# A two-layer decoder with eight experts on one core: the small group's silu is ordered behind the splits of the large group's down weights

## The chip, the core and the metric

The kernel runs on one core of a Trainium2 chip. TensorE (PE, with its weight loads shown apart as PEld) does the matmuls, ScalarE (ACT) and VectorE (DVE) do the elementwise work, GpSimd (POOL) is nearly unused, and SyncE (SP) issues the transfers of the weights from HBM. The metric is the time of the whole kernel on the device in microseconds, as the median of its runs; smaller is better.

## What is computed

Two decoder layers over 256 tokens of width 1024, in float32. Each layer has attention, and then a channel mixer: a dense SwiGLU of inner width 3584 in the first layer, and in the second one eight such SwiGLU experts, of which each token uses two. Of the reference only the mixers matter here:

```python
def swiglu(h, wg, wu, wd):
    return (jax.nn.silu(h @ wg) * (h @ wu)) @ wd

def moe_swiglu(h, router, wg, wu, wd):
    logits = (h @ router).astype(jnp.float32)
    top_vals, top_idx = lax.top_k(logits, TOP_K)          # TOP_K = 2 of 8
    gates = jax.nn.softmax(top_vals, axis=-1)
    ...
    for e in range(N_EXPERTS):
        out = out + gate_e[..., e:e + 1] * swiglu(h, wg[e], wu[e], wd[e])
    return out
```

## The kernel before

The change lies in the second layer's mixer. An expert's tokens are gathered into 128, 64 or 32 slots. Experts are taken in eight turns, 0 to 7. Turns 0, 2, 4, 5 and 6 have 128 slots and are the **large** ones (class `Ffn`); turns 1 and 7 have 64 slots and turn 3 has 32, and these are the **small** ones (class `Few`). Each expert's inner width is cut into seven groups of 512 columns. A group's work is: `gate` (a product over 1024, then silu on ACT), `up` (a product, then a multiplication by the silu on DVE), `turn` (transposes on PE, copied out of PSUM by ACT and, for a large one, by DVE) and `down` (the product with the down weights, summed up in PSUM over the seven groups).

A list of steps, written by hand, mixes the groups: small groups of turn 1 stand among those of 0 and 2, those of turn 3 among 2 and 4 (mostly one small after two large), and those of turn 7 alternate with those of 6. Turn 5 runs alone. A step of group n does `gate(n)`, `turn(n-1)`, `up(n)`, `down(n-1)`. So where a small group follows a large one, PE does in this order: the small gate, the large group's four transposes, the small up, the large group's down.

Weights come as tiles of 1 MiB (128 x 2048 float32), two each for a group's gate, up and down, 336 for the eight experts. They come in a ring of 14 buffers, in the order of use; a tile's transfer is issued when the tile 14 places ahead of it has been used up. A small group multiplies the float32 tile as it is. A large group splits each half of a tile into two parts: ACT writes `whi` (rounded), DVE writes `wlo` (what the rounding left), and PE multiplies three times, `whi` and `wlo` with the high part of the activations and `whi` with the low part. `whi` and `wlo` have four buffers each, so at most four split halves are ahead of PE; a half is six matmuls of 512 columns, so a large gate, up or down has four halves and 24 matmuls.

A scheduler in the tile framework puts each engine's instructions in an order before the program is built. ACT and DVE work through theirs in that order. `tc.issue_after(ins)` is a wish to that scheduler: whatever is recorded in its block comes behind `ins`, if it is on the same engine as `ins`; it adds no wait on a semaphore. The lines that the rows below name are L290 (`whi` on ACT), L291 (`wlo` on DVE), L337 to L339 (the three matmuls), L607 and L616 (silu and multiplication of a large group), L624, L627 and L628 (its transposes, `aTh` on ACT, `aTl` on DVE), L675 (small gate and up), L681 and L684 (silu and multiplication of a small group), L690 and L692 (its transposes and `aTh`) and L702 (small down).

Of the kernel before, what the change touches and what calls it, by code (L numbers as in the profile page):

```python
# [10 lines left out]
F32 = mybir.dt.float32  # L11
# [3 lines left out]
AF = mybir.ActivationFunctionType  # L15
ALU = mybir.AluOpType
# [3 lines left out]
P = 128  # L20
# [76 lines left out]
def trunk(ctx: ExitStack, tc: tile.TileContext, a: dict, out: bass.AP):  # L97
    nc = tc.nc
    V, A, G, T = nc.vector, nc.scalar, nc.gpsimd, nc.tensor
# [160 lines left out]


    ring = [wraw] * RAW
    free, behind = [0], []
    turn = [0]

    def more_raw():
# [14 lines left out]
    def split(raw, shape, q):  # L281
        hi = wsp.tile([P, 1024], F32R, name="whi")
        lo = wsp.tile([P, 1024], F32R, name="wlo")
        half = raw[:, 1024 * q : 1024 * q + 1024]
        with ExitStack() as es:
            free[0] -= 1
            if free[0] < 0:
                for ins in behind:
                    es.enter_context(tc.issue_after(ins))
            A.activation(hi, half, AF.Copy)  # L290
            V.tensor_tensor(lo, half, hi.bitcast(F32), op=ALU.subtract)  # L291
        return [x.rearrange("p (a b) -> p a b", a=shape[0] // 2) for x in (hi, lo)]

    def by_quarter(src, shape):
# [8 lines left out]
    def weight(src, shape):  # L303
        raw = load(src, shape)
        return [split(raw, shape, q) for q in range(2)]

    class Stream:
# [6 lines left out]
        def more(self):  # L314

            while sum(x[1] is not None for x in self.ready) < self.lead and len(self.ready) < 12 + self.lead:
                if not self.raw:
                    t = next(self.tiles, None)
                    if t is None:
                        return  # L320
                    if t[2:] == (QUARTERS,):
                        self.ready += by_quarter(*t[:2])
                        return
                    raw = load(*t[:2])
                    self.raw = [(raw, t[1], q, t[2:]) for q in range(2)]
                raw, shape, q, whole = self.raw.pop(0)
                if whole:
                    half = raw[:, 1024 * q : 1024 * q + 1024]
                    self.ready.append((half.rearrange("p (a b) -> p a b", a=shape[0] // 2), None))
                else:  # L330
                    self.ready.append(split(raw, shape, q))
# [27 lines left out]
    with tc.tile_pool(name="rope0", bufs=1) as rp:  # L359
# [8 lines left out]
        for bits in (8, 9, 9):  # L368
            e = math.floor(math.log2(rest)) + 1 - bits
# [207 lines left out]
    class Ffn:  # L577
# [23 lines left out]
        def gate(self, g):  # L601
            def done(t, ps):
                s = self.s[g, t] = self.sp.tile([P, GW], F32, name="silu", bufs=2 * self.nt)
                if self.rs is None:
                    A.activation(s, ps, AF.Silu)
                else:
                    A.activation(s, ps, AF.Silu, scale=self.rs(t))  # L607
            self.product(self.wg, g, done)
# [46 lines left out]
    class Few:  # L655
# [22 lines left out]

        def gate(self, g):
            s = self.s[g] = self.sp.tile([P, self.nj * P], F32, name="silu", bufs=2)  # L680
            A.activation(s, self.product(), AF.Silu, scale=self.rs)  # L681

        def up(self, g):
            V.scalar_tensor_tensor(self.s[g], self.product(), self.rs, self.s[g], op0=ALU.mult, op1=ALU.mult)  # L684
# [52 lines left out]
    def moe(i, norm, make_next):  # L737
# [74 lines left out]
        with ExitStack() as es:  # L812
            sp = es.enter_context(tc.tile_pool(name=f"mo{i}", bufs=1, reuse_waits="tile"))
            py = es.enter_context(tc.tile_pool(name=f"my{i}", bufs=1, space=PSUM, reuse_waits="tile"))
            xe, oh, ffn, place, of = {}, {}, {}, {}, {}
# [3 lines left out]
            def width(e):  # L819
                return SLOTS[RANKS[e]]  # L820

            def arrange():
# [27 lines left out]
                for src, dst in ((posm, posp), (gate, tokp[:, :, :NE])):  # L850
                    V.tensor_tensor(w, m[:, None].to_broadcast([P, NT, NE, NE]),
                                    src[:, :, None, :].to_broadcast([P, NT, NE, NE]), op=ALU.mult)
                    V.tensor_reduce(dst, w, axis=AX.X, op=ALU.add)
                V.tensor_copy(tokp[:, :, NE : NE + 1], tok[:, :, NE : NE + 1])

            def seat(e):

                oh[e] = [rt.tile([P, P], F32R, name=f"oh{t}") for t in range(NT)]
                for t in range(NT):
                    at = posp[:, t, e : e + 1]  # L860
                    w = width(e)
                    if w < P:
                        V.tensor_scalar(oh[e][t].rearrange("p (b n) -> p b n", n=w),
                                        row[:, None, :w].to_broadcast([P, P // w, w]), at, None, op0=ALU.is_equal)
                    else:
                        V.tensor_scalar(oh[e][t], row, at, None, op0=ALU.is_equal)
# [36 lines left out]
            def places(e):  # L903

                pb = ptr.tile([P, NT, P], F32, name="ps_t")
                for t in range(NT):
                    T.matmul(pb[:, t], (posp if e else posm)[:, t, e : e + 1].to_broadcast([P, P]), ident, start=True, stop=True)
                oT = sp.tile([P, NT, P], F32R, name="oT", bufs=2)
                c = C_COL + WIDTHS.index(width(e))
                V.tensor_scalar(oT, pb, cst[:, c : c + 1], None, op0=ALU.is_equal)  # L910
                place[e] = oT
# [3 lines left out]
            def weigh(e, n2):  # L915
                gs, ps = of[e][:, e : e + 1], ys[e][n2]
                yh = sp.tile([P, 512], F32R, name="yh")
                yl = sp.tile([P, 512], F32R, name="yl")
                A.activation(yh, ps, AF.Copy, scale=gs)  # L919
                V.scalar_tensor_tensor(yl, ps, gs, yh.bitcast(F32), op0=ALU.mult, op1=ALU.subtract)  # L920
                ys[e][n2] = (yh, yl)

            def scatter(e, n2, fed=None):
                (yh, yl), oT = ys[e][n2], place[e]
                cs = slice(512 * n2, 512 * n2 + 512)
                for t in range(NT):
                    pz = ptr.tile([P, 512], F32, name="ps_t")
                    T.matmul(pz, oT[:, t], yh, start=True, stop=False)
                    T.matmul(pz, oT[:, t], yl, start=False, stop=True)  # L929
                    V.tensor_tensor(xs[t][:, cs], xs[t][:, cs], pz, op=ALU.add)  # L930
                    if fed is not None:
                        fed.feed(t, n2)
# [33 lines left out]
            def enter(e):  # L966
                gather(e)
                slots(e)
# [3 lines left out]
            for n, (e, g) in enumerate(steps):  # L972
                over = [x for x in ends if ends[x] + 2 == n]
                if g == 0:
                    rs = of[e][:, NE : NE + 1]
                    if width(e) < P:
                        ffn[e] = Few(lambda k, x=xe[e]: x[:, k], rs, sp, py, stream, width(e), e % 2)
                    else:
                        ffn[e] = Ffn(None, None, None, lambda part, k, t, x=xe[e]: x[:, k, part], 1,
                                     lambda t, rs=rs: rs, sp, py, stream, e % 2)  # L980
                ffn[e].gate(g)
                for x in over:
                    scatter(x, 0)
                    weigh(x, 1)
                if last:
                    with tc.issue_after(ffn[e].mark):
                        ffn[last[0]].turn(last[1])
                ffn[e].up(g)
                if n == 0:
                    arrange()  # L990
                    seat(1)
                if n == 1 or g == NG - 1:
                    if coming < NE:
                        enter(coming)
                        coming += 1
                        if coming < NE:
                            seat(coming)
                    elif e % 2 == 0:
                        fin_g = hpool.tile([P, D], F32, name="mT0")
                        G.dma_start(fin_g, a["final_norm"].partition_broadcast(P))  # L1000
                for x in over:
                    scatter(x, 1)
                if last:
                    ffn[last[0]].down(last[1], lambda t, ps, e=last[0]: ys.update({e: list(ps)}))
                    if last[1] == NG - 1:
                        weigh(last[0], 0)
                if g == NG - 2:
                    places(e)
                last = (e, g)
# [4 lines left out]
            e = NE - 1  # L1014
# [8 lines left out]
        def beyond(write_out):  # L1023
# [4 lines left out]
            with tc.If(full > 0), ExitStack() as es:  # L1028
# [5 lines left out]
                with tc.For_i(0, NE, 1) as ev:  # L1034
# [9 lines left out]
                    for t in range(NT):  # L1044
                        for src, dst in ((posm, slot[:, t : t + 1]), (gate, gt[:, t, 0:1])):
                            pick = sp.tile([P, NE], F32, name="pick", bufs=2)
                            V.tensor_tensor(pick, src[:, t], here, op=ALU.mult)
                            V.tensor_reduce(dst, pick, axis=AX.X, op=ALU.add)
                        V.tensor_copy(gt[:, t, 1:2], tok[:, t, NE : NE + 1])
# [145 lines left out]
```

## Time and profile before

| | |
|---|---|
| median of 3 runs | 1405.68 us (1400.28 to 1405.84) |
| the profiled execution | 1408.49 us |
| its span, first to last instruction | 1406.6 us |
| mean granted clock of PE | 0.984 of full speed |
| PE busy | 1357.5 us, 97% of the span |
| DVE busy | 925.2 us, 66% |
| ACT busy | 783.1 us, 56% |
| read from HBM | 426.80 MB |

A busy PE is a PE with a matmul in flight, not one at its peak: a matmul's end is modelled, so a wait shorter than a matmul's length hardly shows as idle time. Waiting on ACT or DVE costs nothing by itself, since they are not the busiest engines.

### The profile page before, as it was taken

What the parts mean: (1) busy time and instruction counts of PE and PEld (TensorE: products, weight loads), DVE (VectorE), ACT (ScalarE), POOL (GpSimd) and SP (SyncE); (2) the same over time, 40 slices, a digit from 0 to 9 for tenths busy, and PEclk for the clock granted to TensorE, in tenths of its full rate; (3) what the DMA queues carried; (4) which work ended last, traced back from release to release, by engine and by line L of the source; (5) the groups of instructions that cost most, each with busy time, mean ns of one, the idle gap of its engine ahead of it and who ended that gap; (6) DMA issues with size and microseconds to landing.
All of it is one profiled execution on the core that took longest, in us unless ns stands there. A gap on an engine that the chain in (4) does not pass through costs nothing. (4 is left out here: it accounts for less than half of the span.)

```text
span 1406.6 us, 20467 instructions
## 1 busy us (share of the span) xinstructions
PE 1357.5 (97%) x7737; PEld 1041.9 (74%) x7737; DVE 925.2 (66%) x1450; ACT 783.1 (56%) x1118; POOL 7.3 (1%) x17
## 2 busy tenths in 40 slices
PE   7999999999999999999999999999999999999995
PEld 5888888888798787767666777777777786666662
DVE  6887544444787876645546866776689876555444
ACT  6866444444687566544454664666567765544442
POOL 1000000000000000000000000000000000000000
PEclk9999999999999989999999999999999999999997
DMA  8233555544333778999999999999999998999950
GB/s 333 97 144 142 189 182 189 189 186 180 135 146 121 303 295 328 402 420 412 396 409 353 422 420 369 418 421 420 420 420 412 376 356 301 383 403 421 421 239 32
DMA packets 60679, 429.23 MB, mean 305 GB/s; under 512 B 7088, under 2 KB 7280, under 8 KB 8992
## 3 DMA queue, kind: packets, MB, share of 16 engines
q1 hardware_dynamic: 59920, 425.85, 76.2%
q0 software_dynamic: 656, 2.02, 0.4%
q8 instruction: 62, 1.02, 0.3%
q14 instruction: 41, 0.34, 0.1%
HBM read 426.80 MB, written 1.05 MB: 304 GB/s over the span
## 5 line engine op out<-in xcount | busy, mean ns | idle before, releaser
L291 DVE TENSOR_TENSOR wlo<-raw,whi 128x1024 fp32r<-128x1024 f32 x526 | 623.8, 1220 | 165.8 <-ACT whi L290 161.6
L290 ACT ACTIVATE whi<-raw 128x1024 fp32r<-128x1024 f32 x526 | 543.7, 1059 | 242.3 <-PE ps_y L339 123.0
L337 PE MATMUL ps_m<-whi,mT 128*128 128x512 f32 x624 | 251.7, 403 | 0.0
L338 PE MATMUL ps_m<-wlo,mT 128*128 128x512 f32 x624 | 250.1, 401 | 0.1
L339 PE MATMUL ps_m<-whi,mT 128*128 128x512 f32 x624 | 247.9, 397 | 0.0
L338 PE MATMUL ps_y<-wlo,aTh 128*128 128x512 f32 x392 | 159.4, 407 | 16.4 <-DVE wlo L291 16.4
L337 PE MATMUL ps_m<-whi,hT 128*128 128x512 f32 (+1 forms) x416 | 156.3, 377 | 0.9 <-ACT whi L290 0.8
L339 PE MATMUL ps_y<-whi,aTl 128*128 128x512 f32 x392 | 156.7, 401 | 0.0
L338 PE MATMUL ps_m<-wlo,hT 128*128 128x512 f32 (+1 forms) x416 | 155.6, 374 | 0.5 <-DVE wlo L291 0.5
L339 PE MATMUL ps_m<-whi,hT 128*128 128x512 f32 (+1 forms) x416 | 155.2, 373 | 0.0
L337 PE MATMUL ps_y<-whi,aTh 128*128 128x512 f32 x392 | 144.8, 409 | 0.8 <-ACT aTh L627 0.8
L338 PEld LDWEIGHTS ps_m<-wlo,mT 128*128 128x128 f32 x624 | 117.9, 189 | 32.6 <-DVE wlo L291 7.5
L337 PEld LDWEIGHTS ps_m<-whi,mT 128*128 128x128 f32 x624 | 117.8, 189 | 30.9 <-ACT whi L290 3.4
L339 PEld LDWEIGHTS ps_m<-whi,mT 128*128 128x128 f32 x624 | 117.8, 189 | 26.5
L675 PE MATMUL ps_m<-raw,mT 128*64 128x256 f32 (+1 forms) x1664 | 121.4, 328 | 0.0
L675 PEld LDWEIGHTS ps_m<-raw,mT 128*64 128x64 f32 (+1 forms) x1664 | 80.0, 123 | 39.9 <-issue 13.0
L628 DVE TENSOR_TENSOR aTl<-ps_t,aTh 128x512 fp32r<-128x512 f32 x49 | 33.1, 688 | 114.7 <-ACT aTh L627 114.7
L338 PEld LDWEIGHTS ps_y<-wlo,aTh 128*128 128x128 f32 x392 | 75.3, 192 | 41.0 <-DVE wlo L291 23.8
L681 ACT ACTIVATE silu<-ps_m,of 128x256 f32<-128x256 f32 (+1 forms) x21 | 9.2, 438 | 167.6 <-PE ps_m L675 167.6
L337 PEld LDWEIGHTS ps_y<-whi,aTh 128*128 128x128 f32 x392 | 74.2, 193 | 24.7 <-ACT whi L290 4.6
L337 PEld LDWEIGHTS ps_m<-whi,hT 128*128 128x128 f32 x416 | 78.7, 189 | 14.6 <-ACT whi L290 1.2
L338 PEld LDWEIGHTS ps_m<-wlo,hT 128*128 128x128 f32 x416 | 78.7, 189 | 13.8 <-DVE wlo L291 1.0
(215 smaller groups left out, 1282.4 us busy)
## 6 DMA issues: line engine op xcount, KB each, us to landing
raw<-in_moe_w_gate SPq DMA_DIRECT2D x104, 1024.0 KB, 8.8
raw<-in_moe_w_up SPq DMA_DIRECT2D x104, 1024.0 KB, 9.6
raw<-in_moe_w_down SPq DMA_DIRECT2D x103, 1024.0 KB, 9.7
raw<-in_w_in SPq DMA_DIRECT2D x18, 1024.0 KB, 6.5
raw<-in_dense_w_gate SPq DMA_DIRECT2D x14, 1024.0 KB, 4.8
raw<-in_dense_w_up SPq DMA_DIRECT2D x14, 1024.0 KB, 4.8
raw<-in_dense_w_down SPq DMA_DIRECT2D x14, 1024.0 KB, 4.8
raw<-in_w_out SPq DMA_DIRECT2D x8, 1024.0 KB, 4.8
```

The source lines that it names most:

```text
L290: A.activation(hi, half, AF.Copy)
L291: V.tensor_tensor(lo, half, hi.bitcast(F32), op=ALU.subtract)
L337: T.matmul(ps, xh, wh, start=start, stop=False)
L338: T.matmul(ps, xh, wl, start=False, stop=False)
L339: return T.matmul(ps, xl, wh, start=False, stop=stop).ins
L628: V.tensor_tensor(lo, pt, hi.bitcast(F32), op=ALU.subtract)
L675: self.mark = T.matmul(o, self.xT(k), wk[:, b], start=k == 0, stop=k == DK - 1).ins
L681: A.activation(s, self.product(), AF.Silu, scale=self.rs)
```

## The change

`split` keeps its two instructions, the one on ACT and the one on DVE, in a list. The silu of a small group is ordered behind the ACT instruction of the last split recorded so far, and the `turn` of the group before a small one is ordered behind both. When a small gate is recorded, the last split is the fourth half of the large group's down weights. What follows a small group is ordered as before.

```diff
-    free, behind = [0], []
+    free, behind, at_split = [0], [], []
...
-            A.activation(hi, half, AF.Copy)
-            V.tensor_tensor(lo, half, hi.bitcast(F32), op=ALU.subtract)
+            at_split[:] = [A.activation(hi, half, AF.Copy).ins, V.tensor_tensor(lo, half, hi.bitcast(F32), op=ALU.subtract).ins]
...
         def gate(self, g):
             s = self.s[g] = self.sp.tile([P, self.nj * P], F32, name="silu", bufs=2)
-            A.activation(s, self.product(), AF.Silu, scale=self.rs)
+            ps = self.product()
+            with tc.issue_after(at_split[0]):
+                A.activation(s, ps, AF.Silu, scale=self.rs)
...
-                    with tc.issue_after(ffn[e].mark):
+                    with tc.issue_after(ffn[e].mark), ExitStack() as after:
+                        if width(e) < P:
+                            for ins in at_split:
+                                after.enter_context(tc.issue_after(ins))
                         ffn[last[0]].turn(last[1])
```

No instruction is added or removed on any engine, and SP's and POOL's orders stay as they are. What moves stands from the fourth of the 21 small groups on. The line numbers of the changed kernel are one lower up to the small gate's silu, and one higher there.

The first place is ACT's order in the alternation of turns 6 and 7, from the middle of one pair of groups to the middle of the next; L607 is the silu of the large gate, L681 that of the small gate, L627 the large `aTh` and L692 the small one. Before:

```order
L290 ACTIVATE whi<-hT_11276 128x1024 x2
L290 ACTIVATE whi<-raw 128x1024 x2
L607 ACTIVATE silu<-ps_m,of 128x512
L692 ACTIVATE aTh<-ps_t 128x256
L290 ACTIVATE whi<-raw 128x1024 x2
L681 ACTIVATE silu<-ps_m,of 128x256
L627 ACTIVATE aTh<-ps_t 128x512
L290 ACTIVATE whi<-raw 128x1024 x10
```

The same place of the changed kernel, where L606 is the large gate's silu, L682 the small one's, L626 and L693 the two `aTh`:

```order
L290 ACTIVATE whi<-hT_11276 128x1024 x2
L290 ACTIVATE whi<-raw 128x1024 x4
L606 ACTIVATE silu<-ps_m,of 128x512
L693 ACTIVATE aTh<-ps_t 128x256
L290 ACTIVATE whi<-raw 128x1024 x4
L682 ACTIVATE silu<-ps_m,of 128x256
L626 ACTIVATE aTh<-ps_t 128x512
L290 ACTIVATE whi<-raw 128x1024 x6
```

Before, the two splits ahead of the small silu are the last two of the large group's up, and all four of its down stand behind silu and `aTh`. Now all four up splits come ahead of the large gate's silu, and the four down splits ahead of the small gate's.

The second place is DVE's order for the same pair; L684 (L685) is the multiplication of the small up, L616 (L615) that of the large up, L628 (L627) the large `aTl`. Before:

```order
L684 SCALAR_TENSOR_TENSOR silu<-ps_m,of,silu 128x256
L291 TENSOR_TENSOR wlo<-raw,whi 128x1024 x6
L291 TENSOR_TENSOR wlo<-hT_11276,whi 128x1024 x2
L291 TENSOR_TENSOR wlo<-raw,whi 128x1024 x4
L616 SCALAR_TENSOR_TENSOR silu<-ps_m,of,silu 128x512
L628 TENSOR_TENSOR aTl<-ps_t,aTh 128x512
L684 SCALAR_TENSOR_TENSOR silu<-ps_m,of,silu 128x256
```

The changed kernel:

```order
L685 SCALAR_TENSOR_TENSOR silu<-ps_m,of,silu 128x256
L290 TENSOR_TENSOR wlo<-raw,whi 128x1024 x2
L290 TENSOR_TENSOR wlo<-hT_11276,whi 128x1024 x2
L290 TENSOR_TENSOR wlo<-raw,whi 128x1024 x4
L615 SCALAR_TENSOR_TENSOR silu<-ps_m,of,silu 128x512
L290 TENSOR_TENSOR wlo<-raw,whi 128x1024 x4
L627 TENSOR_TENSOR aTl<-ps_t,aTh 128x512
L685 SCALAR_TENSOR_TENSOR silu<-ps_m,of,silu 128x256
```

The four `wlo` of the down weights stood behind the large `aTl` and the small up's multiplication; now they stand ahead of both.

## Rows read from the trace of the kernel before

**Rows 1.** Waits of the whole span: who waited, for whom, total us, times, longest.

```profile
ACT silu L681 <- PE ps_m L675: 167.6, 21, 11.8
PE ps_y L338 <- DVE wlo L291: 16.4, 17, 1.1
```

**Rows 2.** Timeline, all engines, 1255 to 1295: start, us, engine, instruction [idle before].

```profile
1258.25 0.39 PE L337 MATMUL ps_m<-whi,mT 128*128 128x512 f32 x1
...
1270.05 3.65 PE L702 MATMUL ps_y<-raw,aTh 128*64 128x512 f32 x16
...
1273.53 3.62 PE L675 MATMUL ps_m<-raw,mT 128*64 128x256 f32 x32
...
1277.20 0.47 ACT L681 ACTIVATE silu<-ps_m,of 128x256 f32<-128x256 f32 x1 [10.28 <-PE ps_m L675]
...
1278.33 3.88 ACT L290 ACTIVATE whi<-raw 128x1024 fp32r<-128x1024 f32 x4
1278.46 0.69 DVE L628 TENSOR_TENSOR aTl<-ps_t,aTh 128x512 fp32r<-128x512 f32 x1 [7.56 <-ACT aTh L627]
...
1281.39 0.48 DVE L684 SCALAR_TENSOR_TENSOR silu<-ps_m,of,silu 128x256 f32<-128x256 f32 x1 [2.24 <-PE ps_m L675]
1281.79 10.43 DVE L291 TENSOR_TENSOR wlo<-raw,whi 128x1024 fp32r<-128x1024 f32 x9
```

**Rows 3.** Timeline of PE, the large down that follows, 1281 to 1290.

```profile
1281.27 0.73 PE L337 MATMUL ps_y<-whi,aTh 128*128 128x512 f32 x2
1283.06 0.50 PE L338 MATMUL ps_y<-wlo,aTh 128*128 128x512 f32 x1 [1.06 <-DVE wlo L291]
...
1288.30 0.39 PE L337 MATMUL ps_m<-whi,mT 128*128 128x512 f32 x1
```

**Rows 4.** The same stall one pair earlier, timeline of PE, 1240 to 1260.

```profile
1253.02 0.50 PE L338 MATMUL ps_y<-wlo,aTh 128*128 128x512 f32 x1 [1.06 <-DVE wlo L291]
```

**Rows 5.** Timeline, all engines, 600 to 616: a pair of turns 0 and 1.

```profile
602.48 4.62 DVE L291 TENSOR_TENSOR wlo<-raw,whi 128x1024 fp32r<-128x1024 f32 x4
...
608.79 0.47 ACT L681 ACTIVATE silu<-ps_m,of 128x256 f32<-128x256 f32 x1 [5.99 <-PE ps_m L675]
...
614.56 1.06 ACT L290 ACTIVATE whi<-raw 128x1024 fp32r<-128x1024 f32 x1 [4.54 <-DMA raw<-in_moe_w_up]
```

**Rows 6.** Timeline of PE in that pair, 605 to 645.

```profile
612.86 0.50 PE L337 MATMUL ps_y<-whi,aTh 128*128 128x512 f32 x1
...
618.56 0.39 PE L337 MATMUL ps_m<-whi,mT 128*128 128x512 f32 x1
...
630.08 3.65 PE L702 MATMUL ps_y<-raw,aTh 128*64 128x512 f32 x16
```

**Rows 7.** Waits by stretch: 735 to 1030, then two of 1180 to 1385.

```profile
PE ps_y L338 <- DVE wlo L291: 6.9, 8, 1.0
...
PE ps_y L338 <- DVE wlo L291: 7.4, 7, 1.1
...
PEld ps_m L338 <- DVE wlo L291: 2.2, 5, 0.5
```

**Rows 8.** Windows: busy us of PE, PEld, DVE, ACT, POOL; PE clock, DMA share, GB/s.

```profile
655.00:775.00 120.00, 114.91 (x737) 79.16 (x736) 64.01 (x74) 51.91 (x62) 0.00 (x0) 0.99 0.98 388
...
865.00:1075.00 210.00, 205.16 (x1460) 158.91 (x1450) 159.89 (x167) 133.21 (x151) 0.00 (x0) 1.00 1.01 419
...
1225.00:1345.00 120.00, 115.74 (x638) 78.09 (x637) 63.27 (x63) 55.54 (x64) 0.00 (x0) 1.00 1.01 415
```

**Rows 9.** The gate tile in buffer hT, 980 to 1016: issue, time to landing.

```profile
L278 SPq DMA_DIRECT2D hT<-in_moe_w_gate x1: 333/333/333, 983.3 to 983.3; - x1
...
DMA to landing us min/median/max: 19.6/19.6/19.6
```

**Rows 10.** Its first split, timeline of ACT, 1005 to 1018.

```profile
1013.20 1.06 ACT L290 ACTIVATE whi<-hT 128x1024 fp32r<-128x1024 f32 x1 [0.34 <-PE ps_y L339]
```

**Rows 11.** Transfers of raw tiles, 1200 to 1300: us from issue to landing.

```profile
DMA to landing us min/median/max: 4.8/9.3/10.8
```

## The prediction

> **What bounds the kernel now.** I read the page first, then the waits, then the timeline of one pair of groups, then the windows for the transfers. PE is busy for 97% of the span and hardly ever waits for a transfer, so the question is which waits stand on PE's own path in the second layer's mixer. The list of waits has one that repeats: 17 times PE stands before the first `wlo` matmul of a large down (L338 on `ps_y`), waiting for DVE, 16.4 us in all; the small silu on ACT waits 21 times for PE's small gate, 167.6 us in all, 8 us each [rows 1]. The second wait is harmless by itself, but the timeline shows that it makes the first one.
>
> In a pair of turns 6 and 7, PE starts the small gate at 1273.53, and ACT has been idle for 10.28 us when its silu starts at 1277.20. Only behind silu and `aTh` come the four `whi` of the down weights, at 1278.33. DVE is idle for 7.56 us up to `aTl`, then waits another 2.24 us for the small up, and begins its first `wlo` only at 1281.79 [rows 2]. PE reached the down at 1281.27, did the two matmuls that need no `wlo`, and went on at 1283.06 [rows 3]. The tiles had long landed; the splits were merely queued behind instructions that waited for PE.
>
> Here a rule of the Trainium skill is named because it cuts both ways, for the stall above and against the new order (last rival): "PSUM — Partial Sum Buffer", section "Engine vs sequencer instructions", says that the queues of ScalarE and VectorE are strict FIFO. The trace agrees, with 10.28 us of idle ACT in front of four splits.
>
> **What one stall costs.** The kernel itself holds pairs without it. In a pair of turns 0 and 1 the four `wlo` run at 602.48, ahead of the small silu at 608.79 [rows 5]. There the 24 matmuls of the large down take 618.56 - 612.86 = 5.70 us [rows 6]; with the stall they take 1288.30 - 1281.27 = 7.03 us [rows 3]. The stall costs 1.33 us: 1.06 of idle time that the profile counts, and 0.27 more in which PE counts as busy and starts again.
>
> **The change, part by part.**
>
> *The splits ahead of the small silu and of the large turn.* Nothing is added; four `whi` and four `wlo` per small group change places with a silu, an `aTh` and an `aTl`. Do they fit into the idle time? The four buffers for them come free as PE works through the large up, whose last half ends at 1270.05, when the small down begins [rows 2]. Four `whi` take 3.88 us and a `wlo` 10.43 / 9 = 1.16 us [rows 2]; the last `whi` can start at 1270.05 and the last `wlo` ends by about 1270.05 + 1.0 + 1.2 = 1272.3, or 1273 with the large up's multiplication between. That is 4 us before the small gate's result at 1277.20, and 8 us before PE wants the down at 1281.27. So silu, `aTh` and `aTl` keep their times, and the down finds all parts ready. For the pairs with a 32-wide group the gate is shorter, but the split of the last half needs only 2.2 us after the half before it.
>
> So the stall should go in all 17 places. Each is its idle time plus 0.27: 16.4 + 17 x 0.27 = **21.0 us** [rows 1]. By stretches: seven stand in 1180 to 1385 (7.4 us idle, the full 1.33 each), eight in 735 to 1030 (6.9 us, 1.13 each), two before [rows 7]. The lower bound of this term is nothing (the scheduler's wish does not bind the hardware, or another wait fills the place), the upper one is these 21.0. I take the whole, because the undisturbed pair shows exactly this order running with 5.70.
>
> *The large gate's silu, now behind the last two up splits.* In the stalled pair the gate and up of the large group take 1270.05 - 1258.25 = 11.80 us [rows 2]; in the undisturbed pair 630.08 - 618.56 = 11.52 [rows 6]. The 0.28 us belongs to a second, smaller wait for `wlo` that PE's weight loads show five times in 1180 to 1385 [rows 7]; those two splits stand behind the large silu before, and ahead of it now. Between 0 and 14 x 0.28 = 3.9 us for all 14 pairs from 735 on; I take the five that are seen there, **1.4 us**. The silu itself comes about two splits (2 us) later, with an up of 5.6 us to hide it.
>
> *What comes late instead.* A faster PE wants its tiles sooner. A pair of groups is 12 tiles, 12.58 MB. It takes 1283.06 - 1253.02 = 30.04 us now [rows 3, 4] and would take 30.04 - 1.33 - 0.28 = 28.4 us, 443 GB/s, while the transfers bring 415 to 419 with the DMA engines saturated [rows 8]. So the ring must give. In 1180 to 1385: a tile is issued when the one 14 places ahead is used up, 14/12 of a pair = 35 us before its turn, and lands at most 10.8 us later [rows 11], so some 20 us (an estimate from these rows) are in hand once the use of the tile ahead is taken off. Each pair eats 12.58 MB / 419 GB/s - 28.4 = 1.6 us of it; seven pairs eat 11. Nothing comes back there.
>
> It is tighter around 1000, where both the 32-wide pairs and the saturation are. The gate tile in buffer `hT` was issued at 983.3 and landed 19.6 us later, at 1002.9 [rows 9]; its first split started at 1013.20 [rows 10]. PE would be ahead there by the ten stalls before it, 21.0 - 7 x 1.33 = 11.7 us, against 10.3 us in hand. If the transfers gained nothing before, about 1.4 us come back, and up to 4 with the 2.2 us that a half's two splits take. But before 775 they ran below their rate (388 GB/s [rows 8]) because the ring was full, and a faster PE frees it earlier. Between 0 and 4 us come back; I take **1.5**.
>
> **Sum.** 21.0 + 1.4 - 1.5 = 20.9 us less. The profiled execution took 1408.49 us around a span of 1406.6, so it would become 1387.6. That execution is 2.8 us (0.2%) above the median of the runs, 1405.68; the median then becomes 1384.8, and I say **1385 us**, 1.5% faster. About 0.5%, 7 us, is what a measurement of this kernel can tell from no change: its three runs spread over 5.6 us.
>
> **The rivals.**
>
> *The transfers take much of it back.* In the saturated stretches (865 to 1075, and from 1225 on) PE could be held at the rate of the transfers. For it: DMA share 1.01 in both [rows 8], and ACT once waited 4.54 us for a tile [rows 5]. Against it: PE does not wait for a tile there, and even that wait of ACT fell into a down of 5.70 us. If all stalls that lie in those two stretches (I put them at five of the eight of rows 7 and, at 30 us for a pair, five of the seven) were given back, 5 x 1.13 + 5 x 1.33 = 12.3 us, 8.7 would remain: 1397 us.
>
> A rule of the Trainium skill goes further: "DMA: Bandwidth & Descriptors", section "Where 436 GB/s comes from", holds that in transfers from HBM one core's share of it, about 358 GB/s, is what binds. By that rule 352 MB of expert weights need 984 us (an estimate from the page's figure), the whole mixer would hang on HBM, and the change would be worth nothing. The trace differs, with 419 GB/s over 210 us [rows 8], and the measurement decides; a kernel that did hang on its transfers would stay at 1405.7 us, which is the next rival's time and has its chance there.
>
> *Nothing changes.* The wait could pass to another release at the same place, for instance to `aTh` or to the small up's multiplication, which still depend on the small gate. Then PE stands 1.33 us as before, and the time is 1402 to 1409. Against it: in the undisturbed pair those dependences are the same, and the down takes 5.70.
>
> *Slower.* The small silu now stands behind splits that wait for a tile. If a down tile lands after the small gate's end, silu, `aTh` and the large group's down wait with it, where before the late split held up nothing but itself. The trace shows such a queue with the roles the other way round [rows 2]. The place is the stretch before 1010, where landing takes up to 19.6 us. PE has the small up (3.6 us for 64 slots, under 2 for 32) before it needs `aTh`, so it decides when tiles are more than about 1.3 + 3.6 = 5 us late on average. At 7 us late in all of the ten places before 1010, each would lose 2 us instead of gaining 1.2: 10 x 3.2 = 32 of the sum gone, 1385 + 32 = 1417 us. Against it: the margin there was 10 us and shrinks to about zero, not to minus seven.
>
> **How the numbers follow.** Forecast (most stalls gone, 1376 to 1392): 0.74. Transfers take back 7 us or more (1392 to 1399): 0.13. No change (1399 to 1412): 0.09. Slower: 0.04. Of the second case nearly all is still over 0.5% faster (below 1398.7), so faster 0.87, within 0.5% 0.09, slower 0.04. For the range I take 21.0 + 3.9 - 0 = 24.9 us as the most that the terms allow, 1380.8, and 3 us below for the spread of runs, 1378; upward it takes in most of the second case, 1396.
>
> **What the profile of the changed kernel would show.** The row of PE waiting on `ps_y` for `wlo` gone or under 3 us; four `whi` and four `wlo` ended before the small silu in each pair; the large down at 5.70 us everywhere and a pair of turns 6 and 7 at about 28.4 us; the small silu's wait on ACT cut by about 4 us each, to some 100 us; windows from 1200 on at 415 to 422 GB/s without a gap; perhaps a few waits of ACT for a tile around 960 to 1030. I am wrong if `whi` shows long waits for tiles with the small silu right behind them, if the down still takes 7.0 us with another releaser, or if PE's clock falls in more places than now (0.984 on average).

## The result, and the profile after

The changed kernel is slower: 1424.64 us median of four runs (1420.57 to 1428.42) against 1402.98 us of the kernel before on the same chip, a ratio of 1.0145 (95% interval 1.0117 to 1.0173). I had said 1385. The profiled execution of the changed kernel took 1420.57 us around a span of 1418.6, 12.0 more than before. Its mean granted clock is 0.975, where it was 0.984. The spans differ by less than the medians because the profiled execution of before, 1408.49 us, took longer than all four runs above, and that of the changed kernel is the fastest of its four.

The lines have moved a little: `whi` and `wlo` are both L290, the three matmuls L336 to L338, `aTh` and `aTl` of the large turn L626 and L627, the small silu L682, the comparison that makes `oT` in `places` L911 and its matmuls on PE L908, the additions of a scatter L931, the copies of a gather L881 and L894. The page of the changed kernel, its busy times and the group that matters (columns as in the page: line, engine, operation, busy and mean, idle time before it and what ended it):

```profile
PE 1361.9 (96%) x7737; PEld 1050.3 (74%) x7737; DVE 933.9 (66%) x1450; ACT 792.0 (56%) x1118; POOL 7.2 (1%) x17
L338 PE MATMUL ps_y<-whi,aTl 128*128 128x512 f32 x392 | 161.5, 414 | 19.3 <-DVE aTl L627 19.3
L337 PE MATMUL ps_y<-wlo,aTh 128*128 128x512 f32 x392 | 161.5, 412 | 3.1 <-DVE wlo L290 3.1
```

The wait that the change aimed at has shrunk from 16.4 us [rows 1] to 3.1. In its place PE now waits 19.3 us before the next matmul of the same down, the one with `aTl`, a wait that the list of before doesn't have. The list of waits of the changed kernel (who, for whom, total us, times, longest) says how it is spread, and that the small silu's wait went from 167.6 [rows 1] to 79.7 (I had said some 100):

```profile
ACT silu L682 <- PE ps_m L674: 79.7, 18, 6.8
DVE oT L911 <- PE ps_t L908: 27.6, 6, 9.1
PE ps_y L338 <- DVE aTl L627: 19.3, 6, 3.5
```

Six times, 3.2 us each on average. They end at 705, 744, 779, 981, 1207 and 1356 us of the span. The timeline of the last one, ACT, DVE and PE in order of time (start, us, engine, instruction, idle before it):

```profile
1347.61 0.47 ACT L682 ACTIVATE silu<-ps_m,of 128x256 f32<-128x256 f32 x1 [6.78 <-PE ps_m L674]
1348.24 0.60 ACT L626 ACTIVATE aTh<-ps_t 128x512 fp32r<-128x512 f32 x1 [0.16 <-PE ps_t L623]
...
1350.70 0.48 DVE L911 TENSOR_SCALAR oT<-ps_t,cst 128x256 fp32r<-128x256 f32 x1 [6.22 <-PE ps_t L908]
1351.10 4.62 DVE L290 TENSOR_TENSOR wlo<-raw,whi 128x1024 fp32r<-128x1024 f32 x4
...
1352.47 0.50 PE L336 MATMUL ps_y<-whi,aTh 128*128 128x512 f32 x1
...
1352.81 0.40 PE L337 MATMUL ps_y<-wlo,aTh 128*128 128x512 f32 x1
1355.64 0.68 DVE L627 TENSOR_TENSOR aTl<-ps_t,aTh 128x512 fp32r<-128x512 f32 x1
...
1356.38 0.79 PE L338 MATMUL ps_y<-whi,aTl 128*128 128x512 f32 x1 [3.18 <-DVE aTl L627]
...
1356.97 0.63 PE L336 MATMUL ps_y<-whi,aTh 128*128 128x512 f32 x1
```

ACT did its part in time: the `whi` were long done when the small silu ran. DVE did not. It stood idle for 6.22 us, but at the head of its queue was not a `wlo`: it was `oT`, which waits for PE's matmuls of `places`. Only behind it run the four `wlo`, 4.62 us in a row, and only behind all four `aTl`. `aTh` had been ready since 1348.84; `aTl` starts 6.8 us later. PE needs it for its third matmul. Here the rule that I had named, that the queue of VectorE is strict FIFO (the Trainium skill, "PSUM — Partial Sum Buffer", section "Engine vs sequencer instructions"), works against the change, and the trace agrees: four instructions that wait for nothing stand still for 6.22 us behind one that does.

The same place in the kernel before:

```profile
1338.49 0.48 DVE L910 TENSOR_SCALAR oT<-ps_t,cst 128x256 fp32r<-128x256 f32 x1 [7.32 <-PE ps_t L907]
...
1338.90 0.68 DVE L628 TENSOR_TENSOR aTl<-ps_t,aTh 128x512 fp32r<-128x512 f32 x1
...
1343.78 0.50 PE L338 MATMUL ps_y<-wlo,aTh 128*128 128x512 f32 x1 [1.05 <-DVE wlo L291]
```

There `oT` was late too, but `aTl` came right behind it, and PE waited only for one `wlo`.

All the long waits stand in steps of a small group that hold more than gate, up and down: `oT` of `places` (group 5, counted from 0, of turns 1, 3 and 7), a gather (group 6 of turns 1 and 3) or a scatter (group 0 of turns 3 and 7). DVE in the changed kernel, at the gather of turn 1's last step and at the scatter of turn 7's first one: again the instruction ahead of the four `wlo` waits for PE.

```profile
737.09 0.42 DVE L881 COPY mT<-ps_t 128x256 f32<-128x256 f32 x1 [14.33 <-PE ps_t L879]
...
738.77 4.63 DVE L290 TENSOR_TENSOR wlo<-raw,whi 128x1024 fp32r<-128x1024 f32 x4
743.32 0.68 DVE L627 TENSOR_TENSOR aTl<-ps_t,aTh 128x512 fp32r<-128x512 f32 x1
```

```profile
1200.78 0.69 DVE L931 TENSOR_TENSOR x<-x,ps_t 128x512 f32<-128x512 f32 x1 [2.90 <-PE ps_t L930]
1201.39 4.62 DVE L290 TENSOR_TENSOR wlo<-raw,whi 128x1024 fp32r<-128x1024 f32 x4
1205.93 0.68 DVE L627 TENSOR_TENSOR aTl<-ps_t,aTh 128x512 fp32r<-128x512 f32 x1
```

Seven steps are of this kind; from the first matmul of the large down to the first one behind it, these seven take 9.15, 12.78, 12.78, 11.67, 10.63, 13.82 and 11.85 us, 82.7 together, where before it was 48.4: 34 us lost. (In the fifth, PE's down is interrupted by matmuls of the gather; PE waits there 0.82 us for `aTh` and not for `aTl`, and the clock is 0.61 from 1011 to 1024.) The nine quiet steps in which before had the stall show what I forecast everywhere: 5.70 us instead of 6.91 to 7.03, 11.4 us gained, and 1265.58 - 1237.15 = 28.43 us from the down of one pair of turns 6 and 7 to that of the next. The last step of turn 7 went from 7.49 to 5.95 us; with it and the seven, all 17 stalls of [rows 1] are accounted for.

Part of these 34 us is the clock. In the step that ends the list, 11.85 us are 6.15 more than 5.70: PE's second and third matmul start 3.57 us apart instead of 0.23, which is 3.34 us for the wait, and the other 2.81 us come behind it. In windows (us, then busy time of each engine, clock, DMA share, GB/s) around the wait at 1356:

```profile
1340.00:1350.00 10.00, 10.00 (x73) 5.12 (x69) 1.07 (x2) 1.90 (x3) 0.00 (x0) 1.00 1.01 419
1350.00:1357.00 7.00, 3.82 (x26) 2.35 (x25) 6.01 (x7) 0.00 (x0) 0.00 (x0) 0.90 1.01 422
1357.00:1366.00 9.00, 9.00 (x30) 7.12 (x29) 4.06 (x4) 4.31 (x5) 0.00 (x0) 0.70 1.01 421
1366.00:1376.00 10.00, 10.00 (x46) 7.82 (x46) 5.74 (x5) 8.14 (x10) 0.00 (x0) 1.00 0.41 158
```

The granted clock stood at its upper level (2.4 GHz, 1.00) until PE stood idle; for a part of the 9 us behind the wait it was the lower one (1.2 GHz), and then 1.00 again. The Trainium skill ("TensorE: Matmul & The Clock Gate", section "HAM oscillation — how this bites in real kernels") tells of the like for waits on transfers: the next burst starts at the lower clock, each time anew. The trace agrees for this wait, but not for all six (last section). Taken over the span, (1 - 0.975) x 1418.6 = 35.5 us of full speed were not granted, against (1 - 0.984) x 1406.6 = 22.5 before: 13 us more.

### The profile page after: what moved, and what is told of

The parts are those of the page before. It is cut to its first block, busy times and chain, and to the rows that moved or that the text cites. A ratio compares the mean times of both kernels' runs of the same rounds, so it can differ in the third digit from the quotient of the medians.

```text
span 1418.6 us, 20533 instructions
## 1 busy us (share of the span) xinstructions
PE 1361.9 (96%) x7737; PEld 1050.3 (74%) x7737; DVE 933.9 (66%) x1450; ACT 792.0 (56%) x1118; POOL 7.2 (1%) x17
## 4 chain that ended last, share of the span: by engine, by line
PE 92%; DVE 4%; DMA 2%; ACT 1%; issue 1%; SPq 0%; DVEq 0%; ACTq 0%
PE ps_m L337 16%; PE ps_m L336 16%; PE ps_m L338 16%; PE ps_m L674 8%; PE ps_y L338 7%; PE ps_y L336 7%; PE ps_y L337 7%; PE ps_y L703 4%; DVE wlo L290 2%; PE ps_t L623 2%; PE ps_s L459 1%; DMA raw<-in_moe_w_gate 1%; PE ps_t L889 1%; PE ps_pt L483 1%; PE ps_t L879 1%
## 5 line engine op out<-in xcount | busy, mean ns | idle before, releaser
L290 DVE TENSOR_TENSOR wlo<-raw,whi 128x1024 fp32r<-128x1024 f32 x526 | 631.9, 1222 | 200.0 <-ACT whi L290 195.7
L290 ACT ACTIVATE whi<-raw 128x1024 fp32r<-128x1024 f32 x526 | 552.7, 1060 | 348.3 <-PE ps_y L338 202.8
L336 PE MATMUL ps_m<-whi,mT 128*128 128x512 f32 x624 | 251.3, 403 | 0.0
L338 PE MATMUL ps_m<-whi,mT 128*128 128x512 f32 x624 | 247.7, 397 | 0.0
L338 PE MATMUL ps_y<-whi,aTl 128*128 128x512 f32 x392 | 161.5, 414 | 19.3 <-DVE aTl L627 19.3
L336 PE MATMUL ps_y<-whi,aTh 128*128 128x512 f32 x392 | 159.3, 415 | 1.6 <-ACT aTh L626 1.6
L336 PE MATMUL ps_m<-whi,hT 128*128 128x512 f32 (+1 forms) x416 | 156.0, 376 | 1.0 <-ACT whi L290 1.0
L338 PE MATMUL ps_m<-whi,hT 128*128 128x512 f32 (+1 forms) x416 | 154.9, 372 | 0.0
L336 PEld LDWEIGHTS ps_m<-whi,mT 128*128 128x128 f32 x624 | 117.7, 189 | 30.0 <-ACT whi L290 1.7
L338 PEld LDWEIGHTS ps_m<-whi,mT 128*128 128x128 f32 x624 | 117.5, 188 | 27.5
L338 PEld LDWEIGHTS ps_y<-whi,aTl 128*128 128x128 f32 x392 | 77.5, 198 | 40.2 <-DVE aTl L627 21.9
L336 PEld LDWEIGHTS ps_y<-whi,aTh 128*128 128x128 f32 x392 | 77.4, 197 | 25.7 <-issue 5.6
L336 PEld LDWEIGHTS ps_m<-whi,hT 128*128 128x128 f32 x416 | 78.5, 189 | 14.7 <-ACT whi L290 1.4
L338 PEld LDWEIGHTS ps_m<-whi,hT 128*128 128x128 f32 x416 | 78.4, 188 | 13.5
```

Source lines behind the costliest of these rows:

```text
L290: at_split[:] = [A.activation(hi, half, AF.Copy).ins, V.tensor_tensor(lo, half, hi.bitcast(F32), op=ALU.subtract).ins]
L336: T.matmul(ps, xh, wh, start=start, stop=False)
L338: return T.matmul(ps, xl, wh, start=False, stop=stop).ins
```

## The experiments

My theory after this reading: the loss is `aTl`, ordered behind four `wlo` that start late in seven steps because work that waits for PE stands ahead of them on DVE, and the clock that falls in most of these waits. Rival 1: the small silu behind the splits costs it. Rival 2: the transfers take back what a faster PE gains. The kernel before took 1405.22 us beside the first four experiments and 1402.23 us beside the last three (medians on the same chip); the ratios below are against these.

**The small silu's edge alone** (silu_only).

```
-                    with tc.issue_after(ffn[e].mark), ExitStack() as after:
-                        if width(e) < P:
-                            for ins in at_split:
-                                after.enter_context(tc.issue_after(ins))
+                    with tc.issue_after(ffn[e].mark):
                         ffn[last[0]].turn(last[1])
```

> Only the order edge of the small silu stays; the large turn is free again, so aTh and aTl stand ahead of the four whi and wlo, and the small silu and the small up's multiplication behind them. Theory (the loss is aTl queued on DVE behind four wlo that start late in seven steps, plus the clock that falls after each): no wait of PE on aTl is left; wlo no longer waits for the small up, so the wlo wait of PE is mostly gone too, and the large down takes about 5.7 us in the quiet pairs. Time 1380 to 1394 us, faster than before. Rival 1 (the small silu behind the splits is what costs, because the small up and everything behind it come late): about 1415 to 1425 as in the changed kernel. Rival 2 (a faster PE gives all back to the transfers): 1398 to 1406.

Measured: 1383.55 us, ratio 0.9851 (0.9826 to 0.9876), clock 0.987. Rival 1 is out, and so is rival 2: half of the change is faster by 21.7 us, about as much as I had forecast for the whole. The timeline of a pair of turns 6 and 7, ACT and then DVE:

```profile
1259.93 0.60 ACT L626 ACTIVATE aTh<-ps_t 128x512 fp32r<-128x512 f32 x1 [10.92 <-PE ps_t L623]
1260.42 3.89 ACT L290 ACTIVATE whi<-raw 128x1024 fp32r<-128x1024 f32 x4
1264.22 0.46 ACT L682 ACTIVATE silu<-ps_m,of 128x256 f32<-128x256 f32 x1
...
1260.56 0.69 DVE L627 TENSOR_TENSOR aTl<-ps_t,aTh 128x512 fp32r<-128x512 f32 x1 [7.56 <-ACT aTh L626]
1261.51 4.63 DVE L290 TENSOR_TENSOR wlo<-raw,whi 128x1024 fp32r<-128x1024 f32 x4 [0.26 <-ACT whi L290]
1266.06 0.47 DVE L685 SCALAR_TENSOR_TENSOR silu<-ps_m,of,silu 128x256 f32<-128x256 f32 x1
```

Nothing runs in DVE's idle 7.56 us here either. But the small up's multiplication, which in [rows 2] stood ahead of the `wlo` and waited 2.24 us for PE, is now behind them, so the splits no longer wait for the small up. With that the stall is gone: the down takes 5.70 us here.

**The large turn's edges alone** (turn_only).

```
-            with tc.issue_after(at_split[0]):
-                A.activation(s, ps, AF.Silu, scale=self.rs)
+            A.activation(s, ps, AF.Silu, scale=self.rs)
```

> Only the order edges of the large turn stay (aTh behind the last whi, aTl behind the last wlo of the down); the small silu is free and stands ahead of the four whi. Theory: aTl now stands behind silu, four whi and four wlo in every one of some 20 pairs, 4 us or more after PE wants it; with PE's granted clock falling after each, 1440 to 1500 us, far slower than the changed kernel. Rival 1 (the small silu's place is what costs): near before, 1395 to 1410. Rival 2 (transfers decide): within 1% of the changed kernel's 1425.

Measured: 1501.76 us, ratio 1.0687 (1.0658 to 1.0716), clock 0.953; 2 us above the range that I had given. The waits of PE in its list:

```profile
PE ps_y L338 <- DVE aTl L627: 46.4, 16, 3.3
PE ps_y L336 <- ACT aTh L626: 16.9, 13, 2.3
PE ps_y L337 <- DVE wlo L290: 10.0, 10, 1.7
```

The two halves of the change don't add up: 22 us gained and 97 lost, where both together lose 22. ACT's rows in a pair of turns 6 and 7 say why:

```profile
1314.29 0.47 ACT L680 ACTIVATE silu<-ps_m,of 128x256 f32<-128x256 f32 x1 [10.96 <-PE ps_m L674]
1314.66 3.88 ACT L290 ACTIVATE whi<-raw 128x1024 fp32r<-128x1024 f32 x4
1318.44 0.58 ACT L626 ACTIVATE aTh<-ps_t 128x512 fp32r<-128x512 f32 x1
```

The free silu goes to the head and waits 10.96 us for PE, the four `whi` wait with it, and `aTh` behind them. With both edges the `whi` run in that idle time, and `aTh` follows the small silu at once.

**The turn's edges in quiet steps, and in the others** (quiet_only, busy_only). The silu's edge stays everywhere.

```
                 over = [x for x in ends if ends[x] + 2 == n]
+                other = over or g >= NG - 2
...
-                        if width(e) < P:
+                        if width(e) < P and not other:
```

busy_only has `other` in place of `not other`; `other` are the seven steps and the last one of turn 7.

> The edges of the large turn only in steps of a small group that hold no scatter, no gather and follow or issue no places; in the eight other steps aTl is free as before. The small silu's edge stays everywhere. Theory: the quiet pairs keep 28.4 us (nine stalls of about 1.2 less), and the six waits of 3.1 to 3.8 us for aTl are gone, with the clock back to 0.98 or more: 1380 to 1394 us. Rival 1 (the small silu's place): no better than 1415. Rival 2 (transfers give back): 1398 to 1406.

> The opposite choice: the edges of the large turn only in the eight steps of a small group that hold a scatter, a gather or places. Theory: the long waits for aTl stay (six of 3 to 4 us) and the clock falls after them as in the changed kernel, so the time is within 1% of it: 1412 to 1432 us, and slower than quiet_only by 25 us or more. Rival 1 and rival 2: no difference to quiet_only beyond 7 us.

Measured: quiet_only 1381.95 us, ratio 0.9834 (0.9806 to 0.9862), clock 0.987; busy_only 1420.58 us, ratio 1.0114 (1.0089 to 1.0140), clock 0.977. Against silu_only, which has the turn's edges nowhere, those of the quiet steps are worth 1.6 us, less than the runs can tell, and those of the eight others cost 37. In quiet_only no matmul waits for `aTl` any more. The waits of PE in busy_only:

```profile
PE ps_y L338 <- DVE aTl L627: 16.0, 6, 3.5
PE ps_y L337 <- DVE wlo L290: 4.8, 7, 1.7
```

**The other work of DVE behind the splits** (splits_first; silu_work is the same on top of silu_only). The whole change, and in steps of a small group this around the four instructions `oT`, scatter addition and the two gather copies:

```
+                with ExitStack() as es:
+                    for ins in now and at_split[1:]:
+                        es.enter_context(tc.issue_after(ins))
                     V.tensor_scalar(oT, pb, cst[:, c : c + 1], None, op0=ALU.is_equal)
```

(`now` is empty in steps of a large group.)

> The whole change stays, but in steps of a small group the rest of DVE's work that waits for PE (the comparison oT of places, the additions of a scatter, the copies of a gather) is put behind the last wlo recorded so far. Theory (what makes aTl late is not its place behind wlo as such, but that the wlo themselves stand behind work that waits for PE): the four wlo run in DVE's idle time again, aTl follows in time, the long waits for aTl go in most of the seven steps and the clock rises to 0.985 or more: 1376 to 1394 us. Rival (aTl behind four wlo is too late wherever a step holds more work, whatever stands ahead of the wlo): still above 1405.

> The small silu's edge alone, as in silu_only, and DVE's scatter, gather and places work of small steps behind the wlo. Theory: silu_only has no long wait left in these steps (its large downs take 5.7 to 7.0 us), so there is little to gain: 1378 to 1388 us, within 0.4% of silu_only's 1383.6. Rival (the work in front still costs there): under 1376.

Measured: splits_first 1395.66 us, ratio 0.9934 (0.9911 to 0.9956); silu_work 1392.73 us, ratio 0.9923 (0.9896 to 0.9951). Both expectations missed, on the slow side. For `oT` the theory holds: in its three steps the down is back at 5.70 us. The place of the timeline shown above, in splits_first (DVE, then PE):

```profile
1327.12 4.62 DVE L290 TENSOR_TENSOR wlo<-raw,whi 128x1024 fp32r<-128x1024 f32 x4
...
1331.66 0.69 DVE L627 TENSOR_TENSOR aTl<-ps_t,aTh 128x512 fp32r<-128x512 f32 x1
...
1335.20 0.50 PE L336 MATMUL ps_y<-whi,aTh 128*128 128x512 f32 x1
...
1335.77 0.39 PE L338 MATMUL ps_y<-whi,aTl 128*128 128x512 f32 x1
```

Here `aTl` stands behind the same four `wlo` and is ready 2.85 us before the down begins. So its place behind four splits does not make it late by itself; the `oT` ahead of them, which waits for PE, does. For the scatter it went otherwise: its additions hold a `ps_t` buffer that PE needs for the large turn's transposes, and the wait comes back under another name. (The downs of these two steps take 8.04 and 7.72 us: less than 12.78 and 13.82, but not 5.70. The step with the gather of turn 5 got worse, 14.20 us for its down against 10.63; that one I did not take apart.) In splits_first, and in silu_work, where it costs a kernel that had no such wait:

```profile
1188.04 0.66 PE L623 MATMUL ps_t<-cst,silu 128*128 128x128 f32 x4 [3.15 <-DVE x L943]
```

```profile
1182.83 0.66 PE L623 MATMUL ps_t<-cst,silu 128*128 128x128 f32 x4 [3.15 <-DVE x L943]
```

**The wait filled with spare matmuls** (filled). Six steps get, between the first `whi` and the first `wlo` product of the down:

```
+                        spare = pmm.tile([P, 512], F32, name="ps_m")
+                        for k in range(fill[0]):
+                            with tc.issue_after(m.ins):
+                                m = T.matmul(spare, hi[:, c], wh[:, 0, :512], start=k == 0, stop=k == fill[0] - 1)
```

> The whole change stays with its late aTl, but in six of the steps with the long wait (all but the one before the gather of expert 5) PE does 13 to 23 spare matmuls of 0.24 us between the first whi product and the first wlo product of the down, about as long as it stands idle there; their result is not used. Nothing comes earlier, PE just isn't idle. Theory (PE's granted clock falls because PE stands still there): the falls after these six steps go and with them 19 us (worked out as half of 10.24 + 10.24 + 4 x 6.83 less the 10.24 of the seventh): 1400 to 1412 us, clock 0.985 or more. Rival (the clock falls for another reason, or the whole loss is the wait itself): 1418 to 1430 us, clock 0.97 to 0.98.

Measured: 1413.58 us, ratio 1.0077 (1.0046 to 1.0107), clock 0.986. Faster than the changed kernel by 11 us in the medians (7.5 in the profiled spans), with 103 matmuls more to do. It is 1.6 us outside the range given, on the side of the theory. The same place as above:

```profile
1347.85 0.50 PE L647 MATMUL ps_y<-whi,aTh 128*128 128x512 f32 x1
1348.19 3.43 PE L651 MATMUL ps_m<-whi,aTh 128*128 128x512 f32 x14
1351.46 0.40 PE L653 MATMUL ps_y<-wlo,aTh 128*128 128x512 f32 x1
1351.77 0.50 PE L654 MATMUL ps_y<-whi,aTl 128*128 128x512 f32 x1
```

```profile
1350.00:1357.00 7.00, 7.00 (x30) 5.39 (x30) 4.65 (x6) 3.19 (x3) 0.00 (x0) 1.00 1.01 421
1357.00:1366.00 9.00, 9.00 (x41) 7.27 (x40) 7.26 (x6) 7.27 (x9) 0.00 (x0) 1.00 0.91 366
```

PE gets to the `aTl` product at about the same time as without the spare matmuls (3.92 us after the down's start, 3.91 in the changed kernel), but the clock stays at 1.00 where it was 0.90 and 0.70, and the down ends 2.7 us earlier (9.16 against 11.85 us). What full speed is not granted is (1 - 0.986) x 1411.1 = 19.8 us, 15.7 less than in the changed kernel. Not all falls are saved: the one at the gather of turn 5, where nothing was filled in, stays, and the clock fell in a place where it had not in the changed kernel, 1155 to 1175:

```profile
1155.00:1175.00 20.00, 20.00 (x91) 16.73 (x90) 13.83 (x14) 9.41 (x9) 0.00 (x0) 0.83 0.66 259
```

Why it fell there isn't settled; PE was busy in that stretch, with the small matmuls of turn 7's gather. It is no work of the spare matmuls alone: at the same gather the clock also falls in the profiles of before, turn_only, silu_only, quiet_only and silu_work (each 0.89 over 15 us).

## Why the prediction was wrong

**The stall that was to go: right.** PE's wait for `wlo` on `ps_y` went from 16.4 to 3.1 us (I had said gone or under 3), the undisturbed down takes 5.70 us, the pair 28.43 (said: 28.4), the small silu's wait fell to 79.7 (said: some 100). quiet_only, which keeps the change where a step holds nothing else, is at 1381.95 us, and silu_only at 1383.55: the forecast of 1385 was the right size for a kernel without the new wait. The price of a stall was right, too: 1.32 us gained per stall in 1180 to 1385 (said: 1.33), 1.21 in the places of turn 3 (said: 1.13).

**The step that failed** is "So silu, `aTh` and `aTl` keep their times, and the down finds all parts ready", and with it "So the stall should go in all 17 places". I had worked out from one pair, 1255 to 1295, that the four splits fit into DVE's idle time, and took that pair for all. In seven steps DVE's idle time belongs to an instruction that waits for PE and stands ahead of the splits (`oT`, the additions of a scatter, the copies of a gather). There the splits don't fill the idle time, they begin when it ends, and `aTl` moves from ahead of 4.6 us of work to behind it. I priced the moved `aTl` at nothing, with an idle DVE as its cover; where that cover belongs to another wait, it costs 3.2 us six times. Of the term of 21.0 us, 11.4 came in the nine quiet steps and 1.5 in the last one; the other seven, on which I had counted too, lost 34. The rows that would have told it were there: in the list of waits of before, `oT` waits six times for PE, 24.5 us in all, and the additions of the scatters ten times, 9.2 us, and the timeline of before shows one `oT` waiting 7.32 us.

**The rival that I gave 0.04** had the right shape on the wrong engine, and the wrong cause. It let silu, `aTh` and the down come late behind ACT's splits if a tile landed late, and put the price at 2 us in ten places. What came late was `aTl` behind DVE's splits, and no tile made them late but an instruction that waits for PE.

**The second price I had not put in the sum at all:** the clock. I named it last, as a way to be wrong, without a number. In the profiles some 13 us more of full speed were not granted, and the two waits alone add 19.3 - (16.4 - 3.1) = 6.0 us; the span grew by 12.0, so some 7 us were saved in smaller places that I did not take apart. Part of that is luck of the profiled executions: PE's order is the same up to the down of turn 0's group 5, and there the changed kernel is already 4.6 us ahead (637.52 against 642.10). Of these, 2.5 us are one down at 521, where the clock had fallen in the profile of before and not in that of the changed kernel (0.83 and 1.00 from 515 to 535). Counted from that place on, the change costs 16.6 us of span. The runs bear the two prices out from both sides: the waits filled give 11 us back, the waits taken away (quiet_only against the changed kernel) 43.

**The transfers** took nothing back that shows: silu_only and quiet_only gained 21.7 and 23.3 us where I had reckoned 20.9 with 1.5 given back. In the stretch that I had feared for, 865 to 1050, silu_only moves 421 GB/s at a full share of the DMA engines, where the kernel before had 419 [rows 8]:

```profile
865.00:1050.00 185.00, 183.22 (x1317) 141.40 (x1316) 137.86 (x145) 115.90 (x134) 0.00 (x0) 1.00 1.01 421
```

## What to carry to other kernels

An instruction that is ordered behind others inherits every wait in front of them, too. Before moving work "into idle time", look at what stands at the head of that engine's queue in each kind of step, not in one clean pair. An order edge should move the instruction that can afford to be late (the small silu) and leave the one that the bottleneck engine asks for next (`aTl`) where it was; half of this change gave 21.7 of the 23.3 us that the best variant here gained. And a wait on the engine that bounds the kernel should be priced with what the clock does after it.

## What the runs showed of the hardware

A wait of 3.2 us on a PE that was otherwise busy cost more than itself (6.15 us in the step at 1356), and filling six such waits with useless matmuls made the kernel 11 us faster. Behind the wait the matmuls of the changed kernel start 0.43 us apart (1356.97 in the timeline above, then the first row here), with the wait filled 0.23 us (the two rows after it).

```profile
1357.40 0.63 PE L337 MATMUL ps_y<-wlo,aTh 128*128 128x512 f32 x1
```

```profile
1352.10 0.40 PE L336 MATMUL ps_y<-whi,aTh 128*128 128x512 f32 x1
1352.33 0.40 PE L337 MATMUL ps_y<-wlo,aTh 128*128 128x512 f32 x1
```

It does not follow every time: behind the wait at 705 us (its start-to-start gap is 3.3 us longer than usual) the down still took 9.15 = 5.70 + 3.45 us, so its matmuls ran at the upper level. And in the step of the wait that ends at 744 the clock was at the lower level from 738 on, before PE waited for `aTl`. In the four others, which end at 779, 981, 1207 and 1356, it fell while PE stood idle. What tells the one from the others isn't settled here.

The clock can also fall in one execution and not in another at a place where PE does the same: from 515 to 535 us, ahead of everything that these kernels differ in, it is 0.83 in five of the nine profiles and 1.00 in four. A difference of a few us between two profiled spans is therefore not yet one between two kernels.
